# S5's block triangular kernel matrix written by TensorE in one PSUM bank, zeros included

## The chip, the cores and the metric

The kernel runs on one NeuronCore of a Trainium2 chip. The metric is the device time of one execution in microseconds (us); lower is better. A run is compared with runs of the kernel before on the same chip.

## The reference, cut to what matters

The program is a two-layer decoder trunk on 272 tokens (256 and 16 learned meta tokens), width 1024. Each layer runs four token mixers side by side (retention, S5, Mamba-2 SSD, HGRN2), merges them by gates and ends in an MLP. The change touches the S5 mixer alone:

```python
bu_re = jnp.einsum('btgj,gpj->btgp', uf, bb_re)
bu_im = jnp.einsum('btgj,gpj->btgp', uf, bb_im)
...
_, _, xr, xi = lax.associative_scan(combine, (a_re, a_im, bu_re, bu_im), axis=1)
y = (jnp.einsum('btgp,gjp->btgj', xr, c_re.astype(jnp.float32))
     - jnp.einsum('btgp,gjp->btgj', xi, c_im.astype(jnp.float32)))
y = y.reshape(bsz, t, BRANCH_WIDTH) + d_skip.astype(jnp.float32) * u.astype(jnp.float32)
```

It is a diagonal complex recurrence: 32 groups, each with 16 channels in, 64 states, 16 channels out, and a skip `d * u`.

## The kernel before, in words

Weights are streamed: 336 chunks of 128x1024 numbers arrive by DMA in `wst`, ScalarE (ACT) rounds each to `whi` (L326), VectorE (DVE) makes the rest `wlo` (L328), and TensorE (PE) multiplies by three products for each 128 columns of a chunk (L345, L346, L348). These are the "gemm" matmuls; they are most of PE's work. A scheduler of the framework sets each engine's order from priorities and a modelled time line; engines then run their queues in order, with semaphores between them.

S5 takes four tokens at a time (68 steps of four). The 32 groups are handled in four blocks of eight groups, so there are eight blocks in the two layers. Each block is four pairs of groups `q`. For a pair, the output of offset t within four tokens depends on the input of offset s by a 32x32 matrix that depends on t - s alone. `ki` holds these for a pair as a 128x128 block triangular matrix: partitions are 32 for each input offset s, columns 32 for each output offset t; blocks with t < s are zero. Then `s5_run` multiplies `ki` with the input (L1160) and adds the part of the carried state (L1163).

`s5_prep` builds a block's matrices. Its inner function `kd` makes `ki`: for each of four pairs q, PE computes the four 32x32 blocks for t - s = 0 to 3 in 32 rows of the PSUM bank "mc" (L1058 real part, 128 columns; L1059 imaginary part, 128 columns; L1060 adds the skip to the first 32 columns). GpSimd (POOL) clears the three places of zeros in `ki` by memsets (L1062), and ACT copies the blocks to their places four times, for each input offset s into partitions 32s to 32s+31 (L1065). All of it is float32; PE takes a float32 matmul as two records in the trace.

`bank("mc")` has one buffer. It also serves HGRN2's small blocks (`small2`), earlier in each layer. For the first block of layer 1 `s5_prep` is called ahead, in layer 0, and its `kd` is issued by `fill` behind the row sums of the residual.

Of the kernel before, what the change touches and what calls it, by code (L numbers as in the profile page):

```python
# [12 lines left out]
AF = mybir.ActivationFunctionType  # L13
# [6 lines left out]
T = 272  # L20
# [214 lines left out]
class Net:  # L235
# [771 lines left out]
    def s5_prep(self, l, b, after=None):  # L1007

        nc = self.nc
        v, g = nc.vector, nc.gpsimd  # L1010
        pr = slice(4 * b, 4 * b + 4)
        raw = self.s5t("s5a")
        with self.tc.issue_after(after.ins) if after else nullcontext():
            nc.scalar.dma_start(out=raw[:, 0:512], in_=self.io["bc"][l][:, 512 * b:512 * b + 512])
        R4 = raw[:, 0:512].rearrange("p (a q x) -> p a q x", a=4, q=4)

        def outer(e, f, x, out, tmp, r):

            n = f.shape[2]
            sh = [128, 4, n, 32]  # L1020
            F = [f[:, i, :, l, pr].rearrange("p n q -> p q n").unsqueeze(3).to_broadcast(sh) for i in range(2)]
            X = [x[:, i].unsqueeze(2).to_broadcast(sh) for i in range(2)]
            e.tensor_tensor(out=out, in0=X[r], in1=F[0], op=ALU.mult)
            e.tensor_tensor(out=tmp, in0=X[1 - r], in1=F[1], op=ALU.mult)
            e.tensor_tensor(out=out, in0=out, in1=tmp, op=ALU.add if r else ALU.subtract)

        view = lambda a: a.rearrange("p (q n x) -> p q n x", q=4, n=4)

        bs = self.s5t("s5g")[:, 0:1024].rearrange("p (r q n x) -> p r q n x", r=2, q=4, n=4)
        for r in range(2):  # L1030
            outer(v, self.c5, R4[:, 0:2], bs[:, r], view(raw[:, 512:1024]), r)

        slot = [self.s5t(t) for t in ("s5b", "s5c", "s5d")]
        tab = self.s5t("s5e")
        tab2 = slot[2][:, 0:512]
        E = self.s5_table(l, b, tab)
        cx = [c[:, 0:640].rearrange("p (q n x) -> p q n x", q=4, n=5) for c in slot[:2]]
        outer(v, self.pw[:, :, 1:5], R4[:, 2:4], cx[0][:, :, 1:5], view(raw[:, 512:1024]), 0)
        outer(v, self.pw[:, :, 1:5], R4[:, 2:4], cx[1][:, :, 1:5], view(tab2), 1)
        for r in range(2):  # L1040
            nc.scalar.activation(cx[r][:, :, 0], R4[:, 2 + r], AF.Copy)
        st = slot[2][:, 512:1064].rearrange("p (r q c) -> p r q c", r=2, q=4)
        z = [slot[i][:, o:o + 272].rearrange("p (q c) -> p q c", q=4) for i, o in ((0, 640), (1, 768))]
        ki = slot[2][:, 0:512].rearrange("p (q s x) -> p q s x", q=4, s=4)
        bi = self.s5t("s5f")[:, 0:1024].rearrange("p (r q x) -> p r q x", r=2, q=4)
        nb = slot[1][:, 640:768].rearrange("p (q x) -> p q x", q=4)
        nc.scalar.activation(nb, bs[:, 1, :, 3], AF.Copy, scale=-1.0)

        dd = slot[0][:, 912:1040].rearrange("p (q x) -> p q x", q=4)
        for q in range(4):  # L1050
            nc.scalar.activation(dd[:, q], self.c("ident")[:, 0:32], AF.Copy, scale=self.p(l, "s5d", 4 * b + q))

        def kd(pe=nullcontext(), act=nullcontext()):

            kp = self.bank("mc")[0:32].rearrange("p (q d x) -> p q d x", q=4, d=4)
            with pe:
                for q in range(4):
                    nc.tensor.matmul(kp[:, q], lhsT=bs[:, 0, q, 3], rhs=cx[0][:, q, 0:4], start=True, stop=False)  # L1058
                    nc.tensor.matmul(kp[:, q], lhsT=nb[:, q], rhs=cx[1][:, q, 0:4], start=False, stop=False)  # L1059
                    nc.tensor.matmul(kp[:, q, 0], lhsT=self.c("ident")[:, 0:32], rhs=dd[:, q], start=False, stop=True)  # L1060
            for s in range(1, 4):
                g.memset(ki[32 * s:32 * s + 32, :, 0:s], 0.0)  # L1062
            with act:
                for s in range(4):
                    nc.scalar.activation(ki[32 * s:32 * s + 32, :, s:4], kp[:, :, 0:4 - s], AF.Copy)  # L1065

        def bt(pe=nullcontext(), act=nullcontext()):

            tp = [self.bank("mb").rearrange("p (q x) -> p q x", q=4) for r in range(2)]
            with pe:  # L1070
                for r in range(2):
                    for q in range(4):
                        self.turn(tp[r][:, q], bs[:, r, q].rearrange("p s x -> p (s x)"))
            with act:
                for r in range(2):
                    nc.scalar.activation(bi[:, r], tp[r], AF.Copy)

        return (kd, bt), (bi, ki, cx, E, st, z)

    def s5_in(self, l, u):  # L1080
# [490 lines left out]
```

## Time and profile before

| | |
|---|---|
| time, median of 3 runs | 1252.54 us (1251.5 to 1255.18) |
| the profiled execution | 1252.54 us, its span 1250.8 us |
| granted TensorE clock, mean | 0.989 |
| PE busy | 1212.0 us (97%), 9870 matmul records |
| DVE busy | 867.4 us (69%) |
| ACT busy | 692.0 us (55%) |
| POOL busy | 210.7 us (17%) |

The span runs from the first to the last instruction; 1.7 us of the execution's time lie outside it. Busy time is the share in which an engine has at least one instruction under way. A matmul's record is longer than its share of PE, since matmuls overlap: what one costs PE is read from the distance between starts.

### The profile page before, as it was taken

Reading aid. Unit: us, or ns where it says so; the run is one execution under the profiler, and the core shown is the slowest. Engines: PE = TensorE matmul, PEld = TensorE weight load, DVE = VectorE, ACT = ScalarE, POOL = GpSimd, SP = SyncE. Lnnn points to the kernel's source line nnn. Section 1 sums busy time; section 2 is a strip of 40 time slices with the busy share of each in tenths; the row PEclk is TensorE's granted clock in tenths of the full one; section 3 lists DMA queues with packets and bytes.
Section 4 is the critical chain, followed back from the end, with each engine's and each line's share of the span. In section 5 each row is a group of like instructions: output and inputs, shape, how many; then the busy total and the mean of one; then the engine's idle time right before and its main releaser. Section 6 shows DMA issues by size and latency. Waiting matters only on the chain.

```text
span 1250.8 us, 24863 instructions
## 1 busy us (share of the span) xinstructions
PE 1212.0 (97%) x9870; PEld 1175.2 (94%) x9870; DVE 867.4 (69%) x1536; ACT 692.0 (55%) x1231; POOL 210.7 (17%) x289
## 2 busy tenths in 40 slices
PE   8999999999999999999989999999999998999997
PEld 8988899999999989999989998999999997999996
DVE  8699989895637675544468885999555587655443
ACT  8446746544745665544457449456446546665442
POOL 1332102002003142200022232110010032221001
PEclk9999999999999989999989999999999999999998
DMA  7422344434455535555535332444445644665652
GB/s 244 163 86 86 102 141 154 136 107 129 145 170 175 178 104 176 178 171 174 179 101 169 123 102 87 139 158 136 152 135 163 190 155 134 189 187 188 188 184 93
DMA packets 53188, 186.78 MB, mean 149 GB/s; under 512 B 6096, under 2 KB 7248, under 8 KB 53072
## 3 DMA queue, kind: packets, MB, share of 16 engines
q1 hardware_dynamic: 50480, 179.47, 45.2%
q10 hardware_dynamic: 2592, 5.74, 1.4%
q8 instruction: 77, 1.26, 0.4%
q14 instruction: 39, 0.32, 0.1%
HBM read 184.13 MB, written 1.05 MB: 148 GB/s over the span
## 4 chain that ended last, share of the span: by engine, by line
PE 78%; DVE 14%; ACT 4%; issue 2%; DMA 2%; POOL 0%; DVEq 0%; SPq 0%; ACTq 0%
PE g L345 23%; PE g L348 23%; PE g L346 23%; DVE wlo L328 3%; DMA wst<-in_w 1%; ACT whi L326 1%; PE mb L1130 1%; PE mb L731 1%; PE mb L1163 1%; DVE h L609 1%; PE ma L1284 1%; DVE xl_npm L557 1%; DVE S L1293 1%; DVE big_npom L606 1%; DVE big_npost L606 1%
## 5 line engine op out<-in xcount | busy, mean ns | idle before, releaser
L328 DVE TENSOR_TENSOR wlo<-wst,whi 128x1024 fp32r<-128x1024 f32 x336 | 420.4, 1252 | 238.5 <-PE g L348 197.1
L326 ACT ACTIVATE whi<-wst 128x1024 fp32r<-128x1024 f32 x336 | 355.9, 1060 | 352.2 <-PE g L346 284.6
L345 PE MATMUL g<-xh_u,whi 128*128 128x272 f32 (+1 forms) x1024 | 298.7, 292 | 4.9 <-ACT S L663 2.1
L348 PE MATMUL g<-xh_u,wlo 128*128 128x272 f32 (+1 forms) x1024 | 296.0, 291 | 1.6 <-DVE wlo L328 1.5
L346 PE MATMUL g<-xl_u,whi 128*128 128x272 f32 (+1 forms) x1024 | 295.0, 288 | 0.0
L345 PE MATMUL g<-S,whi 128*128 128x272 f32 (+1 forms) x832 | 236.0, 288 | 3.7 <-ACT S L546 3.3
L348 PE MATMUL g<-S,wlo 128*128 128x272 f32 (+1 forms) x808 | 229.9, 288 | 0.7 <-DVE wlo L328 0.7
L346 PE MATMUL g<-S,whi 128*128 128x272 f32 (+1 forms) x768 | 220.3, 289 | 2.2 <-DVE S L557 2.2
L345 PEld LDWEIGHTS g<-xh_u,whi 128*128 128x128 f32 x1024 | 193.7, 189 | 8.8 <-DVE S L691 2.5
L348 PEld LDWEIGHTS g<-xh_u,wlo 128*128 128x128 f32 x1024 | 192.9, 189 | 4.3 <-DVE wlo L328 2.3
L346 PEld LDWEIGHTS g<-xl_u,whi 128*128 128x128 f32 x1024 | 193.7, 189 | 1.1 <-issue 0.6
L345 PEld LDWEIGHTS g<-S,whi 128*128 128x128 f32 x832 | 157.1, 190 | 4.3 <-ACT S L546 3.6
L348 PEld LDWEIGHTS g<-S,wlo 128*128 128x128 f32 x808 | 152.0, 190 | 1.3 <-DVE wlo L328 0.9
L346 PE MATMUL g<-xl_npm,whi 128*128 128x272 f32 (+1 forms) x512 | 147.4, 290 | 2.3 <-DVE xl_npm L557 2.2
L346 PEld LDWEIGHTS g<-S,whi 128*128 128x128 f32 x768 | 146.0, 190 | 3.9 <-DVE S L557 3.6
L345 PE MATMUL g<-xh_npm,whi 128*128 128x272 f32 (+1 forms) x512 | 144.0, 289 | 2.7 <-ACT xh_npm L546 2.7
L348 PE MATMUL g<-xh_npm,wlo 128*128 128x272 f32 (+1 forms) x496 | 142.2, 287 | 0.0
L346 PEld LDWEIGHTS g<-xl_npm,whi 128*128 128x128 f32 x512 | 98.1, 192 | 3.3 <-DVE xl_npm L557 3.1
L345 PEld LDWEIGHTS g<-xh_npm,whi 128*128 128x128 f32 x512 | 96.6, 192 | 3.0 <-ACT xh_npm L546 2.8
L348 PEld LDWEIGHTS g<-xh_npm,wlo 128*128 128x128 f32 x496 | 94.8, 191 | 0.1
L682 POOL TENSOR_TENSOR acc<-acc,tmp 128x272 f32<-128x272 f32 (+1 forms) x48 | 37.2, 788 | 244.6 <-DVE tmp L681 244.6
L365 DVE TENSOR_TENSOR S<-tmp,S 128x272 fp32r<-128x272 f32 (+1 forms) x56 | 25.0, 449 | 62.0 <-ACT S L363 62.0
(387 smaller groups left out, 2021.7 us busy)
## 6 DMA issues: line engine op xcount, KB each, us to landing
wst<-in_w SPq DMA_DIRECT2D x336, 512.0 KB, 3.5
S<-in_rot ACTq DMA_DIRECT2D x4, 544.0 KB, 4.9
s5a<-in_bc ACTq DMA_DIRECT2D x8, 256.0 KB, 3.6
h<-in_h SPq DMA_DIRECT2D x4, 272.0 KB, 4.6
S<-in_ssdc ACTq DMA_DIRECT2D x2, 384.0 KB, 4.3
dtc<-in_ssdc ACTq DMA_DIRECT2D x2, 272.0 KB, 4.6
out<-h SPq DMA_DIRECT2D x2, 256.0 KB, 2.9
cst<-in_cst SPq DMA_DIRECT2D x1, 475.5 KB, 7.4
```

Source lines behind the costliest of these rows:

```text
L326: a = nc.scalar.activation(hi, st, AF.Copy)
L328: nc.vector.tensor_tensor(out=lo, in0=st, in1=hi.bitcast(F32), op=ALU.subtract)
L345: self.nc.tensor.matmul(out, lhsT=a, rhs=r, start=st, stop=False)
L346: self.nc.tensor.matmul(out, lhsT=a, rhs=s, start=False, stop=False)
L348: end = self.nc.tensor.matmul(out, lhsT=b, rhs=r, start=False, stop=en)
L365: nc.vector.tensor_tensor(out=lo, in0=src, in1=hi.bitcast(F32), op=ALU.subtract)
L557: nc.vector.scalar_tensor_tensor(out=nl(k), in0=self.h[:, k, sl], scalar=self.p(l, wname, k), in1=nh(k).bitcast(F32), op0=ALU.mult, op1=AL ...
L606: e.tensor_tensor(out=mw[:, k], in0=mw[:, k], in1=r, op=ALU.mult)
L609: e.tensor_tensor(out=self.h[:, k, sl], in0=self.h[:, k, sl], in1=mw[:, k], op=ALU.add)
L682: nc.gpsimd.tensor_tensor(out=a, in0=a, in1=t, op=ALU.add)
L731: nc.tensor.matmul(out[:, t:T], lhsT=v01[s] if s < 2 else v2, rhs=P[:, p0:p0 + T - t], start=s == 0, stop=s == 2)
L1130: nc.tensor.matmul(vp[:, q], lhsT=bi[:, r, q], rhs=W[:, 4 * b + q], start=True, stop=True)
```

## The change

`kd` uses all 128 rows of the bank "mc". PE first multiplies zeros (a cleared piece of `kpad`) into the places below the diagonal, then, for each pair q, forms every product four times, once for each input offset s, in rows 32s to 32s+31, with 128, 96, 64 and 32 columns. The memsets are gone, and one ACT copy of 128x512 takes the whole matrix.

```diff
-            kp = self.bank("mc")[0:32].rearrange("p (q d x) -> p q d x", q=4, d=4)
+            kp = self.bank("mc").rearrange("p (q d x) -> p q d x", q=4, d=4)
+            rows = [kp[32 * s:32 * s + 32] for s in range(4)]
+            i32 = self.c("ident")[:, 0:32]
+            zero = self.kpad[0][:, 0, T:T + 32].unsqueeze(1)
             with pe:
+                for s in (1, 2, 3):
+                    for q in range(4):
+                        nc.tensor.matmul(rows[s][:, q, 0:s], lhsT=i32, rhs=zero.to_broadcast([128, s, 32]), start=True,
+                                         stop=True)
                 for q in range(4):
-                    nc.tensor.matmul(kp[:, q], lhsT=bs[:, 0, q, 3], rhs=cx[0][:, q, 0:4], start=True, stop=False)
-                    nc.tensor.matmul(kp[:, q], lhsT=nb[:, q], rhs=cx[1][:, q, 0:4], start=False, stop=False)
-                    nc.tensor.matmul(kp[:, q, 0], lhsT=self.c("ident")[:, 0:32], rhs=dd[:, q], start=False, stop=True)
-            for s in range(1, 4):
-                g.memset(ki[32 * s:32 * s + 32, :, 0:s], 0.0)
+                    for s in range(4):
+                        nc.tensor.matmul(rows[s][:, q, s:4], lhsT=bs[:, 0, q, 3], rhs=cx[0][:, q, 0:4 - s], start=True,
+                                         stop=False)
+                    for s in range(4):
+                        nc.tensor.matmul(rows[s][:, q, s:4], lhsT=nb[:, q], rhs=cx[1][:, q, 0:4 - s], start=False,
+                                         stop=False)
+                    for s in range(4):
+                        nc.tensor.matmul(rows[s][:, q, s], lhsT=i32, rhs=dd[:, q], start=False, stop=True)
             with act:
-                for s in range(4):
-                    nc.scalar.activation(ki[32 * s:32 * s + 32, :, s:4], kp[:, :, 0:4 - s], AF.Copy)
+                nc.scalar.activation(ki, kp, AF.Copy)
```

In the changed kernel the zeros are line L1062, the real parts L1066, the imaginary parts L1069, the skip L1072, the copy L1074; every later line is 9 higher than before (L1160 becomes L1169, and so on).

PE, layer 0, second block (`mc_1937` before, `mc_1979` after; rows x columns are those of the output). Before, the twelve matmuls stand in one piece behind gemm matmuls:

```order
L348 MATMUL g_2920<-yh_hg_2440,wlo_2917 128x272
L1058 MATMUL mc_1937<-s5b_1913,s5g_1906 32x128
L1059 MATMUL mc_1937<-s5c_1914 32x128
L1060 MATMUL mc_1937<-s5b_1913,cst 32x32
L1058 MATMUL mc_1937<-s5b_1913,s5g_1906 32x128
L1059 MATMUL mc_1937<-s5c_1914 32x128
L1060 MATMUL mc_1937<-s5b_1913,cst 32x32
```

Now the zeros stand some hundred rows ahead of the rest, behind a matmul of the block before:

```order
L346 MATMUL g_2914<-xl_u_161,whi_2917 128x272
L1169 MATMUL mb_1932<-S_142_1779,s5d_1808 128x68
L1062 MATMUL mc_1979<-kpad_90,cst 32x32 x4
L1062 MATMUL mc_1979<-kpad_90,cst 32x64 x4
L1062 MATMUL mc_1979<-kpad_90,cst 32x96 x4
L345 MATMUL g_2947<-xh_u_160,whi_2950 128x272
```

and the products of the second block follow there with four matmuls for each one before:

```order
L1069 MATMUL mc_1979<-s5c_1956 32x128
L1069 MATMUL mc_1979<-s5c_1956 32x96
L1069 MATMUL mc_1979<-s5c_1956 32x64
L1069 MATMUL mc_1979<-s5c_1956 32x32
L1072 MATMUL mc_1979<-s5b_1955,cst 32x32 x4
L1066 MATMUL mc_1979<-s5b_1955,s5g_1948 32x128
```

The zeros were moved ahead since nothing but the bank holds them back; a block has 60 matmuls where it had 12.

PE, the end of layer 0, where the first block of layer 1 is built ahead (`ma` is the bank of the residual's row sums). Before:

```order
L588 MATMUL ma_4995<-ssq_4994,cst 128x272
L588 MATMUL ma_4995<-sq_5272,cst 128x272
L1058 MATMUL mc_5338<-s5b_3029,s5g_3022 32x128
L1059 MATMUL mc_5338<-s5c_3030 32x128
L1060 MATMUL mc_5338<-s5b_3029,cst 32x32
```

Now:

```order
L588 MATMUL ma_5163<-ssq_5162,cst 128x272
L588 MATMUL ma_5163<-sq_5440,cst 128x272
L1062 MATMUL mc_5506<-kpad_90,cst 32x32 x4
L1062 MATMUL mc_5506<-kpad_90,cst 32x64 x4
L1062 MATMUL mc_5506<-kpad_90,cst 32x96 x4
L1066 MATMUL mc_5506<-s5b_3197,s5g_3190 32x128
```

Here the zeros come right before the products, behind the row sums as before.

## Rows read from the trace of the kernel before

**Rows 1.** The page: busy time, share of the span and instructions by engine.

```profile
PE 1212.0 (97%) x9870; PEld 1175.2 (94%) x9870; DVE 867.4 (69%) x1536; ACT 692.0 (55%) x1231; POOL 210.7 (17%) x289
```

**Rows 2.** Busy us (x instructions) by stretch of the span; then granted clock, DMA share, GB/s.

```profile
core 0: us, PE busy (x) PEld busy (x) DVE busy (x) ACT busy (x) POOL busy (x), PEclk, DMA share, GB/s
100.00:155.00 55.00, 52.27 (x377) 47.68 (x378) 54.24 (x199) 40.38 (x80) 12.53 (x11) 0.97 0.30 92
155.00:295.00 140.00, 136.75 (x1207) 131.54 (x1204) 125.39 (x265) 73.94 (x154) 13.22 (x28) 1.00 0.42 135
800.00:890.00 90.00, 89.37 (x873) 86.81 (x872) 78.30 (x146) 53.47 (x108) 8.46 (x21) 1.00 0.43 142
205.00:225.00 20.00, 17.12 (x138) 16.35 (x138) 19.93 (x40) 12.11 (x21) 0.31 (x2) 1.00 0.41 125
```

**Rows 3.** PE's time line around one block: start us, us, instruction, records.

```profile
870.80 0.39 PE L1058 MATMUL mc<-s5b,s5g 128*32 128x128 f32 x2
871.02 0.38 PE L1059 MATMUL mc<-s5c 128*32 128x128 f32 x2
871.24 0.23 PE L1060 MATMUL mc<-s5b,cst 128*32 128x32 f32 x2
871.30 0.39 PE L1058 MATMUL mc<-s5b,s5g 128*32 128x128 f32 x2
```

**Rows 4.** PE's time line where two records stand alone between gemm matmuls.

```profile
867.52 0.28 PE L345 MATMUL g<-xh_u,whi 128*128 128x256 f32 x1
867.64 0.28 PE L346 MATMUL g<-xl_u,whi 128*128 128x256 f32 x1
867.85 0.41 PE L1058 MATMUL mc<-s5b,s5g 128*32 128x128 f32 x2
868.18 0.38 PE L348 MATMUL g<-xh_u,wlo 128*128 128x256 f32 x1
868.41 0.28 PE L345 MATMUL g<-xh_u,whi 128*128 128x256 f32 x1
```

**Rows 5.** PE's time line around `s5_out` (L1178), which writes four groups of 32 rows in rotation.

```profile
885.59 1.15 PE L1178 MATMUL mb<-S,cst 128*32 128x68 f32 x64
886.67 0.73 PE L1519 MATMUL ma<-S,cst 128*128 128x272 f32 x2
```

**Rows 6.** Groups by line, shapes apart: busy us, mean ns, idle before and its releasers.

```profile
L1076 ACT ACTIVATE s5f<-mb 128x512 f32<-128x512 f32 x16 | 9.2, 594 | 11.2 <-PE mb L701 6.3 <-POOL S L275 4.9
L1065 ACT ACTIVATE s5d<-mc 32x512 f32<-32x512 f32 x8 | 4.7, 585 | 12.6 <-PE mc L1060 11.4 <-issue 1.2
L1065 ACT ACTIVATE s5d<-mc 32x384 f32<-32x384 f32 x8 | 3.8, 481 | 0.1
L1065 ACT ACTIVATE s5d<-mc 32x256 f32<-32x256 f32 x8 | 3.0, 373 | 0.1
L1065 ACT ACTIVATE s5d<-mc 32x128 f32<-32x128 f32 x8 | 2.1, 265 | 0.1
```

**Rows 7.** The same view, shapes together: POOL's memsets.

```profile
L1062 POOL MEMSET s5d<- 32x128 f32 (+2 forms) x24 | 7.4, 307 | 50.8 <-DVE s5c L1025 49.2 <-DVE s5e L1004 1.0
```

**Rows 8.** PE's time line at the end of layer 0, with idle time and releaser.

```profile
436.80 0.22 PE L1060 MATMUL mc<-s5b,cst 128*32 128x32 f32 x2
439.69 0.52 PE L345 MATMUL g<-xh_npm,whi 128*128 128x272 f32 x2 [2.66 <-ACT xh_npm L546]
```

**Rows 9.** Who PE waited for, 155 to 295 us: us in total, times, longest.

```profile
PE g L345 <- ACT S L663: 2.1, 1, 2.1
PE g L348 <- DVE wlo L328: 0.6, 1, 0.6
PE g L345 <- DVE acc L678: 0.2, 1, 0.2
PE mb L1178 <- ACT S L1171: 0.2, 1, 0.2
```

**Rows 10.** PE's time line in layer 1, a wait for POOL.

```profile
833.06 0.70 PE L1486 MATMUL ma<-S,cst 128*128 128x256 f32 x2 [0.63 <-POOL S L1484]
```

## The prediction
> **What bounds the kernel now.** I read the page first: PE is busy 97% of the span, the other engines 17 to 69% [rows 1]. So work that is taken from ACT and POOL and given to PE is suspect from the start, and the question is where PE has room. For that I cut the span into stretches [rows 2]. S5's matrices are built in four places. The zeros of layer 0's first block fall into 100 to 155 us, where DVE is busy 54.24 of 55 us: DVE sets the pace there, PE has room. All else of layer 0 lies in 155 to 295 us: PE 136.75 of 140, DVE 125.39; within it, 205 to 225 us belongs to DVE (19.93 of 20, PE 17.12). Of layer 1, one block is built at the end of layer 0, where PE idles 2.66 us behind it [rows 8]; the zeros of the next fall near 740 us and the last two in 800 to 890 us, where PE is busy 89.37 of 90: no room. The granted clock in the S5 stretches is 1.00, the upper of the two levels.
>
> **The change part by part.**
>
> *The products.* Before, one pair costs PE 871.30 - 870.80 = 0.50 us: two records of 128 columns are 0.22, two of 32 columns 0.06 [rows 3]; four pairs are 2.0 us a block. That is 0.109 us for a record of 128 columns, 1.70 ns per column of a float32 matmul. Now each product is made four times, with 128, 96, 64 and 32 columns, in four different groups of 32 output rows. If the four groups run side by side, the first, with 128 columns, sets the time as before and the others lie beside it: 0 more. If they run in turns, a pair has 2 x 320 + 128 = 768 columns, 1.31 us against 0.50, so 3.2 us a block and 26 us in all. Which one? L1178 writes four groups of 32 rows in rotation too, each matmul 68 columns: 64 records, that is 32 matmuls, take 886.67 - 885.59 = 1.08 us [rows 5], 34 ns a matmul. In turns it would be 68 x 1.70 = 116 ns. So the groups do run side by side, 3.4 deep, and I take 0.
>
> The Trainium skill, "TensorE: Matmul & The Clock Gate", Part 3, says that matmuls start and end strictly in program order, without reordering. By that rule the second record of each matmul would have to wait for the first one of its own group, and everything behind it too. L1178's 1.08 us speak against it: 32 matmuls with one such wait of about 58 ns each would take 1.9 us. What it would do here is the third rival below.
>
> *The zeros.* New on PE: 12 matmuls a block, 4 x 32, 4 x 64 and 4 x 96 columns. They are written group by group (s outside, q inside), not in rotation. Side by side, the longest group sets the time: 384 columns x 1.70 = 0.65 us a block. In turns: 768 columns, 1.31 us. No row shows groups that stand in runs of four, so both ends stay; I take 0.65, since [rows 5] are nearest and show more than one group under way.
>
> *The switching.* Two records alone between gemm matmuls take PE from 867.64 to 868.41, 0.77 us [rows 4]; less two gemm starts of 0.12 and 0.22 for the records themselves, going to 32-row outputs and back costs 0.31 us. The zeros come in nine pieces (one block's are split). Two stand alone; the others lean on small work that interrupts the gemm anyway, and over PE's whole order the number of such interruptions goes from 182 to 183. Each piece so costs between 0 and 0.31; I take the middle, 0.155.
>
> *ACT and POOL.* Four copies, 585 + 481 + 373 + 265 = 1.70 us, become one of 128x512 from PSUM, whose like is L1076, 0.59 us [rows 6]: ACT is rid of 1.1 us a block, 9 us in all. 24 memsets of 0.31 us, 7.4 us, leave POOL [rows 7]. ACT waited for PE in front of the copies, and the memsets sat behind DVE; nothing is shown that waited for either. I credit nothing; the bound of a gain is the fourth rival.
>
> *The wait it adds.* "mc" is now held from the zeros to the copy, and the zeros of the next block, in PE's queue with all gemm behind them, wait for this block's copy. In the order the nearest pair has eight S5 matmuls and nine gemm matmuls between, at least 2 us; the copy starts at once in most blocks and takes 0.59. I take 0. At the far end, a copy that is stuck behind 2 us of other ACT work would cost PE 0.6 us in a block or two.
>
> *The sum.* Six of the nine pieces have no cover: 6 x (0.65 + 0.155) = 4.8 us. The pieces of layer 0's first block are covered by DVE's stretch, the one of layer 1's first block by the idle 2.66 us. Of the six, the third block's zeros of layer 0 stand behind the second block's L1160 at 212 us, in DVE's 20 us: less 0.8. That leaves **+4.0 us**. The profiled execution took 1252.54 us (span 1250.8 and 1.7 outside), which is the median of the runs as well: **1256.5 us**.
>
> **The rivals.**
>
> 1. *Forecast*: side by side, five pieces paid. 1256.5, give or take 2.5. For it: PE's 97%, [rows 5].
> 2. *Most of it hidden.* In 155 to 295 us DVE runs 90% and PE and DVE share the pace, so that PE work put ahead of a wait is free. Only the pieces of 800 to 890 us pay, 2 x 0.8 = 1.6: 1254.1. For it: PE's waits for ACT and DVE there, 3.1 us [rows 9]. Against it: these are four waits, and zeros elsewhere don't meet them.
> 3. *In turns.* The zeros cost 1.31 and a full switch of 0.31, five times: 8.1, so 1260.6. Dearer still is strict order of starts: then the four second records of a product wait in line, 0.109 + 0.082 + 0.055 + 0.029 = 0.275 against 0.218 us, and the skip's four take 0.116 against 0.058; with two products that is 0.17 us a pair, 0.69 a block, and 5 x (1.31 + 0.69 + 0.31) = 11.6: 1264.1. [Rows 5] speak against that one.
> 4. *Faster.* ACT's queue is what makes DVE and PE late in layer 0: PE's longest wait is 2.1 us for L663 on ACT, one more 0.6 for `wlo`, and in layer 1 0.63 for POOL [rows 9, 10]. If those three go (3.3 us) and the 1.1 us less on ACT shortens the queue in each of three blocks of layer 0 (3.3 us), while 1.6 us are paid as in the second rival, it ends at 1252.5 - 5.0 = 1247.5. It decides from the point where ACT's delay, not DVE's, sets 205 to 225 us; against it, DVE is busy 19.93 of these 20 us and ACT 12.11 [rows 2].
>
> That the change does not do what it says is ruled out by PE's order: 60 matmuls a block, no memset, one copy.
>
> What no row bounds is the scheduler: it shifted rows on DVE and ACT all through 155 to 295 us, and a wait of 1 or 2 us may come or go by it. That is in the widths.
>
> **How the numbers follow.** Forecast 0.44, mostly hidden 0.23, in turns 0.13, strict order or all in turns 0.06, faster 0.14. No change means within 0.3%, that is 3.8 us, about what a measurement can tell: 1248.8 to 1256.3. The forecast sits just above it: 0.25 of its 0.44 is slower, 0.19 the same. The hidden case gives 0.22 same and 0.01 slower, the two dear ones 0.19 slower, the faster one 0.13 faster and 0.01 same. Slower 0.45, same 0.42, faster 0.13. The range: 1249 takes in the forecast, the hidden case and the upper end of the faster one; 1262 takes in the zeros in turns and leaves out strict order. About 0.1 is left out on either side.
>
> **What the profile would show.** Right: PE's busy time up by some 5 us with L1062 on PE in eight places, each 0.65 us from first to last start; a pair of products still 0.50 us; L1074 at 0.6 us; no wait of PE for L1074. Wrong: an L1062 set of 1.3 us or a pair of 0.6 to 0.7 (in turns, strict order); PE waiting in front of L1062 for ACT; PE's idle time in 155 to 295 us down by as much as its work is up (hidden), or the waits for L663, `wlo` and L1484 gone and the S5 stretches shorter (faster).

## The result, and the profile after

| | before | after |
|---|---|---|
| median | 1252.02 us (4 runs) | 1260.58 us (4 runs, 1259.08 to 1261.97) |
| the profiled execution, its span | 1252.54, 1250.8 us | 1259.08, 1257.1 us |
| granted clock, mean | 0.989 | 0.991 |

After takes 1.0066 of before's time, 95% interval 1.0051 to 1.0080: 6 to 10 us more, where 4.0 were forecast. The profiled execution of after is the lowest of its four; the traces explain the 6.3 us by which its span is longer. What the median has more, some 2 us, no trace shows.

The page of after, as [rows 1]:

```profile
PE 1219.1 (97%) x10638; PEld 1181.9 (94%) x10638; DVE 867.9 (69%) x1536; ACT 684.9 (54%) x1207; POOL 202.5 (16%) x265
```

PE is busy 7.1 us longer, ACT 7.1 and POOL 8.2 us less. By stretch, as [rows 2] (span, then busy us of PE, PEld, DVE, ACT, POOL):

```profile
155.00:295.00 140.00, 138.09 (x1550) 132.72 (x1548) 124.42 (x264) 70.09 (x141) 7.85 (x13) 1.00 0.43 137
740.00:800.00 60.00, 57.39 (x452) 52.37 (x452) 37.11 (x57) 42.67 (x83) 11.89 (x11) 1.00 0.34 108
```

In layer 0's stretch PE's idle time fell from 3.25 to 1.91 us. In 740 to 800 us it now has 2.6 us of idle time, where before has almost none,

```profile
740.00:800.00 60.00, 59.95 (x466) 55.52 (x465) 43.06 (x70) 43.62 (x86) 11.58 (x12) 1.00 0.35 110
```

and in 800 to 890 us it is busy all 90.00.

**Where the time went.** Two matmuls that every kernel has serve as marks on PE: the last L1276, ahead of S5's work in layer 1, and the last L1519, behind it. A row gives the shortest, median and longest duration in ns, then the first and last start in us. Before:

```profile
L1276 PE MATMUL ma<-S,S x32: 222/222/270, 96.9 to 738.9; 128*64 128x64 f32 x32
L1519 PE MATMUL ma<-S,cst x16: 390/392/497, 257.9 to 899.3; 128*128 128x272 f32 x16
```

After (each line 9 higher):

```profile
L1285 PE MATMUL ma<-S,S x32: 222/222/270, 97.3 to 740.2; 128*64 128x64 f32 x32
L1528 PE MATMUL ma<-S,cst x16: 390/392/393, 268.0 to 906.2; 128*128 128x272 f32 x16
```

PE is 1.3 us late at the first mark and 6.9 at the second: the four blocks of layer 0 and the one built ahead at its end cost 1.3 us net, the three of layer 1 behind the mark 5.6.

**The zeros.** PE's time line around a set of twelve that stands alone:

```profile
850.65 0.28 PE L345 MATMUL g<-yh_hg,whi 128*128 128x256 f32 x1
850.85 1.25 PE L1062 MATMUL mc<-kpad,cst 128*32 128x32 f32 x24
852.04 0.39 PE L346 MATMUL g<-yl_hg,whi 128*128 128x256 f32 x1
852.26 0.28 PE L348 MATMUL g<-yh_hg,wlo 128*128 128x256 f32 x1
```

From the first zero to the next gemm matmul 1.19 us; the whole detour 852.26 - 850.65 = 1.61, less two gemm starts of 0.12: 1.37 us.

**The products.** A whole block of them, and inside it the change from one pair to the next:

```profile
819.91 0.28 PE L345 MATMUL g<-xh_u,whi 128*128 128x256 f32 x1
...
820.63 0.28 PE L1066 MATMUL mc<-s5b,s5g 128*32 128x128 f32 x3
820.68 0.20 PE L1069 MATMUL mc<-s5c 128*32 128x32 f32 x1
...
820.75 0.27 PE L1066 MATMUL mc<-s5b,s5g 128*32 128x128 f32 x1
...
821.13 0.28 PE L1066 MATMUL mc<-s5b,s5g 128*32 128x128 f32 x3
...
822.23 0.38 PE L346 MATMUL g<-xl_u,whi 128*128 128x256 f32 x1
```

A pair is 821.13 - 820.63 = 0.50 us, as in [rows 3], with four times the matmuls.

**A new wait.** Who PE waited for, 735 to 910 us:

```profile
PE g L345 <- DVE S L691: 2.4, 1, 2.4
```

The wait for L691 is new there (besides it the list has only 0.2 us for L1469), and L1484's 0.63 [rows 10] is gone. The chain of waits through it (start, us, what):

```profile
780.87 2.09 DVE S L749
782.95 1.52 DVE wlo L328
...
784.93 2.56 DVE S L769 x2
787.49 0.34 DVE S L691
...
787.87 0.39 PE g L345
```

L691 reads the gemm's PSUM bank `g` that PE wants next, and DVE's queue has two L769 of 1.28 us ahead of it. In 155 to 295 us the four waits of [rows 9], 3.1 us, are gone; in their place stands one:

```profile
PE mb L1187 <- ACT S L1180: 1.8, 1, 1.8
```

L1074 was never waited for by PE (median 598 ns, eight copies).

### The profile page after: what moved, and what is told of

The parts are those of the page before. It is cut to its first block, busy times and chain, and to the rows that moved or that the text cites. A ratio compares the mean times of both kernels' runs of the same rounds, so it can differ in the third digit from the quotient of the medians.

```text
span 1257.1 us, 26343 instructions
## 1 busy us (share of the span) xinstructions
PE 1219.1 (97%) x10638; PEld 1181.9 (94%) x10638; DVE 867.9 (69%) x1536; ACT 684.9 (54%) x1207; POOL 202.5 (16%) x265
## 4 chain that ended last, share of the span: by engine, by line
PE 82%; DVE 11%; ACT 4%; issue 1%; DMA 1%; POOL 0%; SPq 0%; DVEq 0%; ACTq 0%; POOLq 0%
PE g L345 24%; PE g L348 24%; PE g L346 24%; DVE wlo L328 2%; PE mb L1139 1%; ACT whi L326 1%; PE mb L1172 1%; PE mb L731 1%; DVE h L609 1%; PE ma L1293 1%; DMA wst<-in_w 1%; DVE xl_npm L557 1%; DVE S L1302 1%; PE mb L701 1%; DVE big_npom L606 1%
## 5 line engine op out<-in xcount | busy, mean ns | idle before, releaser
L328 DVE TENSOR_TENSOR wlo<-wst,whi 128x1024 fp32r<-128x1024 f32 x336 | 419.0, 1248 | 237.1 <-PE g L348 193.7
```

Source lines behind the costliest of these rows:

```text
L328: nc.vector.tensor_tensor(out=lo, in0=st, in1=hi.bitcast(F32), op=ALU.subtract)
```

## The experiments

Theory A: the zeros' own time on PE is the loss; products are free, relief of ACT and POOL is worth nothing. Rival B: the order that the scheduler moved, with new waits, is the loss. Rival C: the relief gives something back and hides a larger cost. All kernels ran in turn with the kernel before; the marks are those of their own profile, against 738.9 and 899.3 us. A mark comes from one execution: after, 1, 9 and 12 share the order of layer 0 and stand at 1.3, 1.4, 2.4 and 1.9 us at the first one, so a mark is good to about 1 us.

| kernel | median us | to before, 95% | late at first mark | at second | between |
|---|---|---|---|---|---|
| after | 1260.58 | 1.0066, 1.0051 to 1.0080 | 1.3 | 6.9 | 5.6 |
| 1 zeros rotated | 1259.29 | 1.0054, 1.0039 to 1.0070 | 1.4 | 6.2 | 4.8 |
| 2 products four times, no zeros | 1256.03 | 1.0032, 1.0020 to 1.0044 | 0.7 | 3.0 | 2.3 |
| 3 zeros added to before | 1261.82 | 1.0074, 1.0060 to 1.0088 | 1.2 | 10.9 | 9.7 |
| 4 zeros once | 1254.93 | 1.0018, 1.0008 to 1.0028 | -1.6 | 2.4 | 4.0 |
| 5 zeros between pairs | 1256.89 | 1.0040, 1.0028 to 1.0052 | -2.0 | 4.0 | 6.0 |
| 6 zeros behind products | 1258.12 | 1.0045, 1.0033 to 1.0057 | 1.1 | 5.4 | 4.3 |
| 7 as 5, s5_out later | 1254.68 | 1.0018, 1.0009 to 1.0028 | -1.6 | 1.5 | 3.1 |
| 8 as 2, s5_out later | 1258.06 | 1.0053, 1.0040 to 1.0067 | 0.1 | 5.2 | 5.1 |
| 9 changed in layer 0 only | 1255.11 | 1.0017, 1.0008 to 1.0026 | 2.4 | 2.9 | 0.5 |
| 10 changed in layer 1 only | 1259.69 | 1.0054, 1.0041 to 1.0067 | -0.2 | 5.4 | 5.6 |
| 11 as 5, layer 0 only | 1251.43 | 0.9987, 0.9979 to 0.9996 | -0.9 | -0.8 | 0.1 |
| 12 one block held | 1258.28 | 1.0044, 1.0031 to 1.0058 | 1.9 | 5.6 | 3.7 |

### 1. Zeros rotated

```diff
-                for s in (1, 2, 3):
-                    for q in range(4):
+                for q in range(4):
+                    for s in (1, 2, 3):
                         nc.tensor.matmul(rows[s][:, q, 0:s], lhsT=i32, rhs=zero.to_broadcast([128, s, 32]), start=True,
```

> The changed kernel with the zeros' two loops exchanged, so that the three row groups take turns; the order of DVE, ACT, POOL and SP is the same to the row, and PE's differs in these 96 matmuls alone. Theory A (the lost time is the zeros' own time on PE): a set alone takes 0.65 to 0.75 us from first to last start where it took 1.07, so 0.35 us less for each of the pieces that pay, three in layer 1 and up to four in layer 0: 1 to 2.5 us under the changed kernel, 1258 to 1259.5. Rival B (the moved order with its new waits makes the loss): the order is the same, so no difference over 0.5 us, 1260.6.

PE's time line around the set that stood alone in after:

```profile
850.61 0.86 PE L1062 MATMUL mc<-kpad,cst 128*32 128x32 f32 x24
851.40 0.39 PE L346 MATMUL g<-yl_hg,whi 128*128 128x256 f32 x1
```

0.79 us against 1.19, 0.40 less a set. In rotation the groups lie side by side; in runs of four they do so only in part. Between the marks 0.8 us went, and the medians differ by 1.3, within their intervals. The wait for L691 is the same 2.4 us. A's part is real and small.

### 2. Products four times, no zeros

```diff
-                for s in (1, 2, 3):
...
+            for s in range(1, 4):
+                g.memset(ki[32 * s:32 * s + 32, :, 0:s], 0.0)
             with act:
-                nc.scalar.activation(ki, kp, AF.Copy)
+                for s in range(4):
+                    nc.scalar.activation(ki[32 * s:32 * s + 32, :, s:4], rows[s][:, :, s:4], AF.Copy)
```

> The products four times as in the changed kernel, but no zeros on PE: POOL's memsets and ACT's four copies stay as before. Theory A: the products lie side by side and cost 0, a pair stays at 0.50 us: 1252.5, within 1.5. A rival, that four times as many matmuls cost something beyond their columns: a pair of 0.6 us or more, 3 us and more in all, 1255.5 or over. Rival B: PE's cost is as before, but the order is changed, so waits of 1 to 3 us come or go: up to 1257.

A's 1252.5 was missed by 3.5 us, though the products are free in this trace too: a block without its first real-part product takes 1.89 us from its first matmul to the next gemm matmul, in before and here. The time is in a wait, on PE (here L1185 is `s5_out`, L1178 its GELU):

```profile
828.84 0.28 PE L346 MATMUL g<-yl_hg,whi 128*128 128x256 f32 x1
831.52 1.15 PE L1185 MATMUL mb<-S,cst 128*32 128x68 f32 x64 [2.40 <-ACT S L1178]
```

and on ACT:

```profile
828.19 1.05 ACT L326 ACTIVATE whi<-wst 128x1024 fp32r<-128x1024 f32 x1
...
829.52 1.28 ACT L1178 ACT_TABLE_LOAD   x1
830.81 0.66 ACT L1178 ACTIVATE S<-S 128x544 f32<-128x544 f32 x1
```

Before, the same place on PE:

```profile
830.46 0.28 PE L348 MATMUL g<-yh_hg,wlo 128*128 128x256 f32 x1
830.72 1.16 PE L1178 MATMUL mb<-S,cst 128*32 128x68 f32 x64
```

Before, 21 gemm matmuls on `yh_hg` stood ahead of `s5_out`; here two, and ACT has a rounding and L690 ahead of the GELU. Part of B holds: an order that moved costs 2.4 us with no zeros at all. With 0.7 us for L678 and without before's 0.6 for L1484, waits make 2.5 us, and 2.3 went between the marks. The theory from here on has two causes, the zeros' time and moved waits.

### 3. Zeros added to the kernel before

```diff
...
+                for s in (1, 2, 3):
+                    for q in range(4):
+                        nc.tensor.matmul(full[32 * s:32 * s + 32, q, 0:s], lhsT=self.c("ident")[:, 0:32],
+                                         rhs=zero.to_broadcast([128, s, 32]), start=True, stop=True)
                 for q in range(4):
                     nc.tensor.matmul(kp[:, q], lhsT=bs[:, 0, q, 3], rhs=cx[0][:, q, 0:4], start=True, stop=False)
```

(`full` is the whole bank, `kp` its first 32 rows as before.)

> The kernel before, with the twelve matmuls of zeros added into rows of the bank that nobody reads; memsets and four copies stay. Theory A: all of the loss is here, 1258 to 1262 (six or seven pieces of 1.1 to 1.4 us less what DVE's stretches cover), a set alone again 1.07 us. Rival B: three pieces pay in layer 1 and the rest is hidden, 1254 to 1257. Rival C (ACT's and POOL's relief gives back 2 us or more in the changed kernel): 1262 and over.

The zeros alone cost as much as the whole change: 1261.82 and 1260.58 us lie within each other's intervals. Its profile, the slowest of its six executions, loses 9.7 us between the marks. Its longest waits there:

```profile
PE g L345 <- DVE S L691: 2.4, 1, 2.4
PE ma L1492 <- POOL S L1490: 1.2, 1, 1.2
PE g L348 <- DVE wlo L328: 0.6, 1, 0.6
```

The wait for L691 comes with the zeros near 742 us again. Behind it the granted clock is 0.84 in 785 to 790 us and 0.82 in 790 to 795, which is 1.7 us of the 9.7 (an estimate: 0.16 and 0.18 of 5 us); after, with the same wait, has 1.00 there. The two waits below it are not in after. The time lies at A's upper end, just under C's bound; whether ACT's and POOL's relief or the order spares after those waits is not separated. At the first mark it is 1.2 us late, as after is: in layer 0 the relief shows no gain.

### 4. Zeros once

```diff
-            kp = self.bank("mc").rearrange("p (q d x) -> p q d x", q=4, d=4)
+            kp = self.kbank.rearrange("p (q d x) -> p q d x", q=4, d=4)
-                for s in (1, 2, 3):
...
+        self.kbank = self.bank("mc")
...
+        nc.vector.memset(self.kbank, 0.0)
```

(the bank's other two users take `self.kbank` as well.)

> The bank is held for the whole program and cleared once at the start; products four times and one copy as in the changed kernel, no zeros on PE later. Theory A with relief worth nothing: 1251 to 1253. Rival C: ACT's 9 us and POOL's 7.4 us less are worth something, 1250 or under. Rival B: the order decides, 1254 and over with waits of PE of 2 us or more that the kernel before has not.

PE is 1.6 us ahead at the first mark, then loses 4.0, with 0.5 us of waits for L680 and this one in front of `s5_out` (L1184):

```profile
PE mb L1184 <- ACT S L1177: 2.8, 1, 2.8
```

Behind it the granted clock is 0.66 in 830 to 835 us. B's case: no zeros on PE, free products, and slower by waits and by the clock behind them.

### 5. Zeros between pairs

```diff
-                for s in (1, 2, 3):
...
                     for s in range(4):
-                        nc.tensor.matmul(rows[s][:, q, s], lhsT=i32, rhs=dd[:, q], start=False, stop=True)
+                        last = nc.tensor.matmul(rows[s][:, q, s], lhsT=i32, rhs=dd[:, q], start=False, stop=True)
+                    with self.tc.issue_after(last.ins):
+                        for s in (1, 2, 3):
+                            nc.tensor.matmul(rows[s][:, q, 0:s], lhsT=i32, rhs=zero.to_broadcast([128, s, 32]), start=True,
+                                             stop=True)
```

> The changed kernel, but a pair's zeros come right behind that pair's products (one matmul for each of three row groups, held there by a dependence on the pair's skip), not ahead. The groups below the first have fewer columns of products, 64, 128 and 192 less in a pair, and the zeros need 32, 64 and 96, so they fit beside the first group. Theory now: two causes, the zeros' time on PE (some 3 us in layer 1) and waits of PE that the moved order brings (2.5 us for L691 near 785 us in every kernel with zeros near 742 us, or 2.4 us in front of s5_out near 829 us in those without). Then: a block's products and zeros take 2.1 to 2.3 us in one piece as the products alone do, no wait for L691 at 785, but the wait in front of s5_out of 2 to 3 us, since its place in PE's order is that of the second experiment: 1254 to 1256.5. If the zeros cost their own time wherever they stand: 1257 and over, pieces of 2.5 us and more.

A block's products without the first real part, and all its zeros (L1071):

```profile
810.16 0.31 PE L1065 MATMUL mc<-s5c 128*32 128x128 f32 x6
...
811.80 0.33 PE L1071 MATMUL mc<-kpad,cst 128*32 128x64 f32 x5
...
812.06 0.38 PE L346 MATMUL g<-xl_u,whi 128*128 128x256 f32 x1
```

The same piece before, without zeros:

```profile
812.57 0.41 PE L1059 MATMUL mc<-s5c 128*32 128x128 f32 x2
...
814.46 0.38 PE L348 MATMUL g<-xh_u,wlo 128*128 128x256 f32 x1
```

1.90 us against 1.89: between the pairs the zeros cost nothing. Yet the kernel loses 6.0 us between the marks, and its waits there (L1180 the GELU, L1493 a product on POOL) are, the whole list,

```profile
PE mb L1187 <- ACT S L1180: 1.9, 1, 1.9
PE ma L1495 <- POOL S L1493: 1.6, 1, 1.6
PE g L345 <- DVE acc L678: 0.6, 1, 0.6
```

4.1 us, where before has 0.6 [rows 10]; no wait for L691 at 785. That leaves 2.5 of the 6.0 us, and they go with a lower clock. Behind the first two waits (columns as above; the granted clock is the third number from the end):

```profile
830.00:835.00 5.00, 3.85 (x16) 3.67 (x17) 1.83 (x5) 0.80 (x3) 1.10 (x1) 0.50 0.50 170
835.00:840.00 5.00, 5.00 (x138) 4.84 (x136) 2.25 (x4) 2.87 (x5) 0.79 (x2) 0.82 0.22 52
```

0.50 is the lower of the two levels, 1.2 GHz; gemm matmuls start 0.21 us apart in place of 0.12 until 836.66 us. From 831.15 us that costs some 2.8 us (an estimate: half of the 5.5). In 800 to 890 us before and after are at 1.00. The median, 1256.89 us, lies between the two ranges expected. The lead of 2.0 at the first mark, as the fourth's 1.6, is the first sign of a gain in layer 0.

### 6. Zeros behind products

```diff
-                for s in (1, 2, 3):
...
+                with self.tc.issue_after(first.ins):
+                    for s in (1, 2, 3):
+                        for q in range(4):
+                            nc.tensor.matmul(rows[s][:, q, 0:s], lhsT=i32, rhs=zero.to_broadcast([128, s, 32]), start=True,
+                                             stop=True)
```

(behind the products; `first` is the first of them.)

> The changed kernel, but a block's twelve zeros come behind its products, group by group as in the changed kernel, held there by a dependence. Theory (zeros' own time and moved waits): pieces of 2.1 + 0.9 to 1.1 us, so 3 us paid in layer 1, no wait for L691 at 785, the wait in front of s5_out of 2 to 3 us as in the second experiment: 1257 to 1260, over the fifth experiment by 2 to 4 us. If the early place of the zeros is the whole loss: 1253 or under.

The end of a piece, 813.31 to 816.13 us (L1074 the zeros):

```profile
813.31 0.31 PE L1067 MATMUL mc<-s5c 128*32 128x128 f32 x6
...
815.10 1.11 PE L1074 MATMUL mc<-kpad,cst 128*32 128x32 f32 x20
816.13 0.38 PE L346 MATMUL g<-xl_u,whi 128*128 128x256 f32 x1
```

2.82 us, 0.92 over the fifth's 1.90: the same zeros, group by group and last, are paid. The time is as expected, 1.2 us over the fifth where 2 to 4 were expected: at the same place its waits for the GELU and for POOL are 1.1 and 1.5 us, and the clock stays at 1.00.

### 7 and 8. `s5_out` later

To the fifth and to the second kernel, in layer 1 (`kdm` is the last real-part product of the third block; the GELU stays behind the second block):

```diff
+            if l and b == 2:
+                with self.tc.issue_after(self.kdm.ins):
+                    outs = self.s5_out(Y, None)
+                for i, ps in enumerate(outs):
+                    nc.scalar.activation(yf[:, i], ps, AF.Copy)
             self.s5_run(l, b, W, prep, Y[:, 4 * (b % 2):4 * (b % 2) + 4])
```

> The fifth experiment with one thing more: in layer 1 the first s5_out is written behind the third block's preparation and held behind its first products, so it stands ten gemm matmuls later in PE's order, and ACT does its GELU before the next rounding, not after. Theory: the wait of PE in front of s5_out falls from 2 to 3 us to under 0.7, and the time with it: 1251 to 1254, within 0.2% of the kernel before; this is the version that could beat it. If the wait in front of s5_out hid other lateness: the same wait elsewhere and 1254 to 1256.5.

> The second experiment (products four times, no zeros on PE, memsets and four copies as before) with the same later place of layer 1's first s5_out in PE's order. Its ACT order keeps a rounding ahead of the GELU. Theory (products free, the second experiment's 3.6 us are the wait in front of s5_out and what follows it): that wait falls from 2.4 us to 0 to 1.3 and the time to 1252 to 1254.5. If the products themselves cost the 3.6 us: 1256, unchanged.

The wait for the GELU is gone in both. In the seventh the next instruction in PE's queue waits for POOL instead:

```profile
PE ma L1507 <- POOL S L1505: 2.4, 1, 2.4
```

and in the eighth

```profile
PE ma L1505 <- POOL S L1503: 3.8, 1, 3.8
```

The theory's expectation is missed in both; the seventh ended as its alternative says, the eighth 2 us over its own. `s5_out` was only first in line. PE's order suggests a cause ahead of it: of the gemm matmuls on `yh_hg` that cover this place in before, all but two now stand behind it; no run moved them back alone. Behind these waits the granted clock is 0.66 in 830 to 835 us in the seventh, and 0.73 and 0.59 in the two stretches of 5 us from 830 in the eighth, where the second has 1.00. That moving one instruction can lengthen the wait (2.4 to 3.8 us; 1256.03 to 1258.06, intervals that just overlap) speaks for B once more.

### 9 and 10. One layer at a time

```diff
+            if l == 0:
                 kp = self.bank("mc").rearrange("p (q d x) -> p q d x", q=4, d=4)
...
+            else:
+                kp = self.bank("mc")[0:32].rearrange("p (q d x) -> p q d x", q=4, d=4)
```

(with `l == 1` in the tenth; the other branch is the body of before.)

> The changed kernel's form for layer 0's four blocks, the form of before for layer 1's four. Layer 0's order is the changed kernel's, layer 1's is that of before around L691 and the first s5_out. Theory (the loss sits in layer 1; layer 0's zeros are nearly paid by waits that went away there): behind on the kernel before by 1.0 to 1.5 us at 300 us and by the same at the end, no wait of 2 us or more in 740 to 900 us: 1253 to 1254.5. If the loss is spread over all the pieces that pay, as forecast (half of them in layer 0): 1255.5 to 1257.5.

> The other half: the form of before in layer 0, the changed one for layer 1's four blocks. Theory: equal to the kernel before until 740 us, then the zeros near 742 us with the wait of 2.4 us for L691 near 785 us, and two more pieces: behind by 5 to 5.8 us from 900 us on: 1257 to 1259. If the loss is spread evenly: 1255.5 to 1257.

The halves add up: 0.17% and 0.54% against 0.66%. Between the marks the ninth loses 0.5 us and the tenth 5.6, all of after's. The ninth is a little over its expectation, 1255.11, and in its profile PE is 2.4 us late at the first mark and not 1.3. The tenth is 0.7 us over its own. In the tenth PE waits 2.4 us for L691 again, in the ninth it does not.

### 11. Zeros between pairs in layer 0 only

The fifth kernel's body under `if l == 0`, that of before under `else`.

> The fifth experiment's form (zeros right behind each pair's products) in layer 0 only, the form of before in layer 1. In the fifth experiment PE stood 1.7 to 2.1 us ahead of the kernel before from 300 to 800 us and lost 6 us in 820 to 900 us, with waits that came from the moved order there. Theory: layer 1's order is now that of before and so is its time; the lead of layer 0 stays to the end: 1249.8 to 1251.2, the version that beats both. If the lead was chance of one profile or is lost again in layer 1: 1252 to 1253.

PE is 0.9 us ahead at the first mark and 0.8 at the second. At 1251.43 us it is the only kernel under before, by 0.04 to 0.21%, though 0.2 us over the range expected; it is one of twelve intervals, and its lead at the marks is no more than a mark is good to. Its zeros have the form that cost PE nothing in the fifth, and the wait for L663 of [rows 9] is not in its list for 155 to 295 us. Whether ACT's relief or the order took that wait away is open: the second and eighth, without relief, have no lead (0.7 and 0.1 late), the fourth, fifth and seventh, with it, have 1.6 to 2.0, but their order differs as well.

### 12. One block's zeros held

```diff
+                if (l, b) != (1, 1):
+                    zeros()
...
+                if (l, b) == (1, 1):
+                    with self.tc.issue_after(last.ins):
+                        zeros()
```

(`zeros` is after's loop; the second `if` stands behind the products.)

> The changed kernel with one thing undone: the zeros of layer 1's second block alone (those near 742 us) come behind that block's products, not 70 us ahead. Up to that place every engine's order is the changed kernel's; behind it DVE has L691 again between L769 and L328 as in the kernel before, and layer 1's first s5_out stands where it stands in the second and fifth experiments. Theory (the wait of 2.4 us for L691 near 785 us comes from the order that the early zeros brought, not from the zeros' time): no wait for L691 over 0.5 us; PE is ahead of the changed kernel by 3.5 to 4.2 us at 800 us (the wait and one piece of 1.4 us); then the piece's zeros come back with 1.1 us behind the products, and the wait in front of s5_out of 1 to 2.6 us: 1.0 to 2.5 us under the changed kernel at the end, 1258 to 1259.6. If the wait for L691 has another cause: it stays at 2.4 us, and the time at 1260 to 1261.

Who PE waited for, 735 to 910 us, the whole list:

```profile
PE ma L1501 <- POOL S L1499: 0.7, 1, 0.7
```

and DVE's time line there:

```profile
782.87 0.47 DVE L769 SCALAR_TENSOR_TENSOR S<-S,half,S 128x256 f32<-128x256 f32 x1
783.27 0.41 DVE L691 SCALAR_TENSOR_TENSOR S<-S,g 128x256 f32<-128x256 f32 x1
783.72 1.07 DVE L769 SCALAR_TENSOR_TENSOR S<-S,half,S 128x256 f32<-128x256 f32 x1
```

L691 stands between the L769 again, as in before (there at 781.05, 781.44 and 781.89 us), and the wait is gone: it came from the order that the early zeros brought. This was the cleanest pair, since up to 742 us DVE, ACT and POOL run the order of after. The wait in front of `s5_out` that was expected did not come; between the marks it loses 3.7 us, about what three sets cost (0.92 behind the products, two of some 1.4).

## Why the prediction was right, and its size not

The range and the sign held; the forecast of +4.0 us met +6.3 in the span of the profiled execution (6.5 in its time) and 6 to 10 in the runs. That the median, 1260.58, is the third rival's 1260.6 is luck: that sum has five sets at 1.62 and no new wait. Step by step:

- *Products, 0:* right. The pair stays at 0.50 us, the pieces at 1.89 and 1.90 us (experiments 2 and 5).
- *Zeros, 0.65 side by side:* mis-sized, 1.07 from first to last start. The working kept both ends and took the lower since [rows 5] were nearest; but those rows rotate the groups and the zeros don't. From the first start to the next gemm matmul, 0.65 would have been 0.77 and in turns 1.43; it is 1.19. Rotated it is 0.79, so the price was right for the other loop order.
- *Switching, 0.155:* mis-sized for a set alone. 1.37 us for the detour less 1.07 (1.19 less one gemm start) leaves 0.3, the upper end, as [rows 4] had it. A lone set so costs 1.37 us and not 0.805.
- *Cover:* three sets in layer 1 have none, as said: at most 4.1 us, since the sets near 742 and 825 us each have small work on one side and only the one at 851 stands alone. Layer 0 was charged 1.6 and paid 1.3, but not by the way given: PE's work there grew and waits of 3.1 us went while one of 1.8 came. So zeros were paid by waits that went, as the second rival has it, and these are the waits that the fourth names.
- *The added wait for the copy, 0:* right, none is in the lists.
- *Relief of ACT and POOL, nothing:* no gain in after (the third experiment, zeros without relief, is as late at the first mark). The waits for L663, `wlo` and L1484 did vanish as the fourth rival named them, and were outweighed.
- *The scheduler:* the step that failed. "A wait of 1 or 2 us may come or go by it" stood in the widths and not in the sum; one of 2.4 us came, for L691. Experiment 12 shows the cause.

The sum with measured terms: 1.3 for layer 0, then 3 x 1.37 + 2.4 - 0.6 (L1484's wait) = 5.9 against 5.6 between the marks; 0.6 is won behind them, which no experiment took up. In the same way (all waits less before's 0.6, the sets at their price, and 1.7, 1.7, 2.8, 1.7 and 2.9 us for the lower clock in 3, 4, 5, 7 and 8, estimates) the other kernels come out within 0.5 us of what they lose between the marks, the eighth 1.0 too high.

## What to carry to other kernels

On a full engine whose order a scheduler writes, twelve matmuls a block cost by where they stand: between pairs whose shorter groups leave room the zeros were free (1.90 us with them and without), in a place of their own 1.37 us a set. Read what a moved order did to the waits before blaming the instructions: kernels with no extra PE time lost 2 to 6 us between the marks, part of it where the clock fell behind a wait. Where a change pays in one stage and loses in another, apply it to the one: layer 0 alone gave the only kernel under before, by 0.13% (0.04 to 0.21).

## What the runs showed of the hardware

- Matmuls with 32 output rows in different groups start out of program order. In after, a record of L1069 with 32 columns starts at 820.68 us, ahead of one of the same pair's L1066 with 128 columns at 820.75, which stands before it in the program. The Trainium skill, "TensorE: Matmul & The Clock Gate", Part 3, has all matmuls start in program order; here the measurement decides. Strict order would have made a pair 0.67 us by the third rival's working where it is 0.50.
- How far groups overlap depends on how they are mixed: the same twelve zeros take 1.19 us in runs of four and 0.79 in rotation, nothing between pairs.
- A wait of PE can cost more than itself. The granted clock fell to its lower level behind waits of 1.9 and 1.6 us (experiment 5), 2.8 (4), 2.4 (7 and, for L691, 3) and within one of 3.8 us (8), for some 2 to 3 us of lost time; behind the 2.4 us in after, 1, 2 and 10 it stayed at 1.00.
- L769 on DVE takes 0.47 us at one time and 1.0 to 1.3 at another, and L328 1.2 or 2.1, in before and in experiment 12 as well. The two L769 of 1.28 us ahead of L691 in after lie beside this work on POOL:

```profile
784.81 2.40 POOL L1471 TENSOR_TENSOR S<-S,early 128x432 f32<-128x432 f32 x2 [0.88 <-ACT S L1470]
```

  The Trainium skill, "GPSIMD Engine Reference", 1 "Specifications", has POOL share its SBUF interfaces with VectorE, with contention for DVE instructions of two SBUF inputs; the rows agree, and no run took POOL's work away from there.
